# One hybrid decoder layer: GpSimd's instructions kept in the order of the program

## The chip, the cores and the metric

The kernel runs on one core of a Trainium2 chip. The metric is the device time of one execution in microseconds (us), lower is better. Its engines are TensorE (PE in the profile), VectorE (DVE), ScalarE (ACT), GpSimd (POOL) and SyncE (SP, which only issues transfers here). Each engine works through its own queue of instructions in order and waits where an instruction's semaphore is not there yet.

## The reference, cut to what matters

One layer on 256 tokens, model width 1024, in float32. A combined projection of the normed input gives group A's queries, keys and values (8 heads of 64) and group B's latents with a shared rotary key. Group A's queries and keys are normed by head, group B's after their up-projections, where 32 of 96 columns are rotated by the token's position.

```python
xn = rms_norm(h, norm_mix_g)
proj = jnp.einsum('bsd,de->bse', xn, w_in)
qa, ka, va, c_q, c_kv, k_rope = jnp.split(proj, cuts, axis=-1)
qa = rms_norm(qa.reshape(b, s, N_HEADS_A, HEAD_DIM_A), qnorm_a_g)
ka = rms_norm(ka.reshape(b, s, N_HEADS_A, HEAD_DIM_A), knorm_a_g)
out_a = dilated_attention(qa, ka, va, rel_bias).reshape(b, s, WIDTH_A)
...
kb = rms_norm(kb, knorm_b_g)
qb = jnp.concatenate([qb[..., :QK_NOPE_DIM], apply_rope(qb[..., QK_NOPE_DIM:], positions)], axis=-1)
kb = jnp.concatenate([kb[..., :QK_NOPE_DIM], apply_rope(kb[..., QK_NOPE_DIM:], positions)], axis=-1)
...
h = h + jnp.einsum('bse,ed->bsd', mixed, w_o)
hid = jnp.square(jax.nn.relu(jnp.einsum('bsd,df->bsf', hn, w_ff1)))
h = h + jnp.einsum('bsf,fd->bsd', hid, w_ff2)
```

## The kernel before

Every product is made of three: an operand is split into a high part, which TensorE takes exactly, and the rest (`his`, `los`), and high x high, low x high and high x low are summed in PSUM. For weights ScalarE writes the high part (L243) and DVE the low one (L244, called a split below), in pieces of up to 1024 columns, in rings of `PARTS` = 5 buffers; the weights come in by SyncE's queue into a ring of three `raw` buffers. Transposed activations are split in the same way with the norm's gain (L275, L276).

TensorE's order is written out by hand in `STEPS` and held by `keep_in_program_order`, which `Products._issue` calls for each product and transpose. A letter is a kind of step: `p` projects group A's queries and keys, `c0` and `c1` the query latent, `l` the key-value latent, `A` transposes and stacks group A's heads (`stack_heads`), `L` transposes the latents, `x` makes a unit of group A's scores and probabilities, `y` transposes one, `r` is the rotary tables. The other engines' instructions are put in order by a scheduler that simulates the timeline; only at the start, while `starting` is set, ScalarE's and DVE's are pinned too.

The work of GpSimd:

- fills of constants: `ident`, `mhalf` (L260), `causal` (L437, L438) and the zeros of `q_lo` (L447);
- the input's norm factor (`ssx`, `rstd`, `eps_x`, L358 to L363) and the products of gains `qk_a`, `qk_b`, which read `cols`;
- group A's four powers: `normed_heads` has ScalarE square a projection, DVE sum it by head (`head_sums`, L460, into `s_a`), GpSimd scale the sum (L484) and raise it to -1/2 (`rsqrt`, L266), and DVE multiply (L487). `s_a00` and `s_a01` belong to the queries, `s_a10` and `s_a11` to the keys, for the two halves of the tokens;
- the rotary tables (`rotary_tables`, L371 to L421): some 60 small operations on 32 or 64 columns, nearly all in one chain, with three on DVE in it (L398, L401, L403);
- later the latents' norm factors, the rotation of the shared key (L616 is its last step), and group B's powers.

`stack_heads` for the keys ends on DVE with L506, which frees the PSUM bank (`mm`, two of them) that the transposes of the next step need. L501 is the same for the queries, L540 the division of group A's probabilities.

Of the kernel before, what the change touches and what calls it, by code (L numbers as in the profile page):

```python
# [16 lines left out]
F32 = mybir.dt.float32  # L17
F32R = mybir.dt.float32r
I32 = mybir.dt.int32
AF = mybir.ActivationFunctionType  # L20
ALU = mybir.AluOpType
AX = mybir.AxisListType

P = 128
S = 256
# [3 lines left out]
H = 8  # L29
DA = 64  # L30
# [13 lines left out]
MASK = 1e29  # L44
# [104 lines left out]
class Products:  # L149


    def __init__(self, tc):
        self.tc = tc
        self.in_order = True
# [8 lines left out]
        return self._issue(self.tc.nc.tensor.transpose(**kw))  # L163


@with_exitstack
def tile_layer(ctx, tc, x, xt, cols_in, rows_in, w_all, out):
    nc = tc.nc
    V, A, G, T = nc.vector, nc.scalar, nc.gpsimd, Products(tc)

    const = ctx.enter_context(tc.tile_pool(name="const", bufs=1))
    keep = ctx.enter_context(tc.tile_pool(name="keep", bufs=1))
    big = ctx.enter_context(tc.tile_pool(name="big", bufs=2))
    two = ctx.enter_context(tc.tile_pool(name="two", bufs=3))
# [173 lines left out]
    load(out=rows, in_=rows_in)  # L348
    starting.clear()

    def sumsq(src, dst):
        junk = sqs.tile([P, DM], mybir.dt.bfloat16, name="sqs")
        return A.activation(out=junk[:, :src.shape[1]], in_=src, func=AF.Square, accum_out=dst)  # L353

    ssx = tiny(NT, "ssx")
    for t in range(NT):
        sumsq(xs[t], ssx[:, t:t + 1])
# [75 lines left out]
        A.dma_start(out=vec_d, in_=vec)  # L433
        A.dma_start(out=bias_r, in_=bass.AP(tensor=vec_d.tensor, offset=vec_d.offset, ap=[[1, P], [NDIST, H], [1, S]]))

    causal = const.tile([P, S], F32, name="causal")
    G.memset(causal, 0.0)  # L437
    G.affine_select(out=causal[:, P:], in_=causal[:, P:], pattern=[[-1, P]], compare_op=ALU.is_ge, fill=MASK, base=0, channel_multiplier=1)  # L438

    k_st = big.tile([P, H // 2, 2, S], F32R, name="big")
    q_st = two.tile([P, 2, H // 2, 2, S], F32R, name="two")
    q_hi, q_lo = q_st[:, 0], q_st[:, 1]
    own = (slice(0, DA), slice(DA, P))
    for i in range(2):
        G.memset(q_lo[own[1 - i], :, i, :].bitcast(F32), 0.0)  # L447
    va, vb = ([keep.tile([P, H, DV], F32, name=f"{n}{t}") for t in range(NT)] for n in ("va", "vb"))


# [133 lines left out]
    def have_cq(b, ps):  # L584
        for t in range(NT):
            V.tensor_copy(out=cn[t][:, b * 384:(b + 1) * 384], in_=ps[t][:, :384])
            sumsq(cn[t][:, b * 384:(b + 1) * 384], ssc[:, b * NT + t:b * NT + t + 1])
# [6 lines left out]
    def have_ckv(ps):  # L594
        for t in range(NT):
            V.tensor_copy(out=cn[t][:, QR:], in_=ps[t][:, :KVR])
            V.tensor_copy(out=kr[t], in_=ps[t][:, KVR:KVR + ROPE])
            sumsq(cn[t][:, QR:], ssc[:, 2 * NT + t:2 * NT + t + 1])
            sumsq(kr[t], ssc[:, 3 * NT + t:3 * NT + t + 1])

        G.tensor_tensor(out=ssc[:, NT:2 * NT], in0=ssc[:, 0:NT], in1=ssc[:, NT:2 * NT], op=ALU.add)
        for i, n in enumerate((QR, KVR)):
            sl = slice(i * NT, (i + 1) * NT)
            G.tensor_scalar(out=mc[:, sl], in0=ssc[:, (i + 1) * NT:(i + 2) * NT], scalar1=1.0 / n, scalar2=None, op0=ALU.mult)
            G.tensor_tensor(out=mc[:, sl], in0=mc[:, sl], in1=eps_x, op=ALU.add)
        rsqrt(fc, mc, 2 * NT)
        G.tensor_scalar(out=eps_q, in0=mc[:, 0:NT], scalar1=EPS, scalar2=None, op0=ALU.mult)
        G.tensor_tensor(out=by_kr, in0=rstd, in1=rstd, op=ALU.mult)
        G.tensor_tensor(out=add_k, in0=ssc[:, 3 * NT:], in1=by_kr, op=ALU.mult)
        G.tensor_scalar(out=add_k, in0=add_k, scalar1=1.0 / DB, scalar2=EPS, op0=ALU.mult, op1=ALU.add)  # L610
        G.tensor_tensor(out=add_k, in0=add_k, in1=m_kv, op=ALU.mult)
        G.tensor_tensor(out=by_kr, in0=m_kv, in1=f_kv, op=ALU.mult)
        G.tensor_tensor(out=by_kr, in0=by_kr, in1=rstd, op=ALU.mult)
        for t in range(NT):
            rotate(G, kr[t].unsqueeze(1), tabs[1], t)
            G.tensor_scalar(out=kr[t], in0=kr[t], scalar1=by_kr[:, t:t + 1], scalar2=None, op0=ALU.mult)  # L616
# [108 lines left out]
    for step in STEPS.split():  # L725
        name, _, times = step.partition("*")
# [137 lines left out]
```

## Time and profile before

| what | us |
|---|---|
| three runs | 324.32, 325.64, 325.48 |
| their median | 325.48 |
| the profiled execution | 324.74 |
| its span, first to last instruction | 322.9 |
| TensorE busy | 311.2 |
| DVE busy | 216.0 |
| ScalarE busy | 177.7 |
| GpSimd busy | 62.5 |

Times in the views are counted from the span's start. A busy share is a mean over the whole span; which wait ends last in a stretch is read from the waits and from the order of time in that stretch.

### The profile page before, as it was taken

What the parts mean: (1) busy time and instruction counts of PE and PEld (TensorE: products, weight loads), DVE (VectorE), ACT (ScalarE), POOL (GpSimd) and SP (SyncE); (2) the same over time, 40 slices, a digit from 0 to 9 for tenths busy, and PEclk for the clock granted to TensorE, in tenths of its full rate; (3) what the DMA queues carried; (4) which work ended last, traced back from release to release, by engine and by line L of the source; (5) the groups of instructions that cost most, each with busy time, mean ns of one, the idle gap of its engine ahead of it and who ended that gap; (6) DMA issues with size and microseconds to landing.
All of it is one profiled execution on the core that took longest, in us unless ns stands there. A gap on an engine that the chain in (4) does not pass through costs nothing.

```text
span 322.9 us, 4547 instructions
## 1 busy us (share of the span) xinstructions
PE 311.2 (96%) x1646; PEld 266.1 (82%) x1646; DVE 216.0 (67%) x387; ACT 177.7 (55%) x317; POOL 62.5 (19%) x118
## 2 busy tenths in 40 slices
PE   8989779989999999999999999999999999999995
PEld 7867679968998887788888888888888888888883
DVE  4673869986887997357887484574764845845722
ACT  5866246977885677328674463453544544535500
POOL 6889960170336200000200000000000000000000
PEclk9999997999999999999999999999999999999999
DMA  7994748434461473212848556465637364563002
GB/s 241 405 346 149 253 112 300 154 116 132 144 202 62 137 255 130 80 52 74 319 144 296 212 151 239 164 219 156 239 134 256 137 211 179 169 222 130 0 35 97
DMA packets 12326, 56.95 MB, mean 176 GB/s; under 512 B 1384, under 2 KB 3440, under 8 KB 7696
## 3 DMA queue, kind: packets, MB, share of 16 engines
q1 hardware_dynamic: 10560, 54.94, 49.4%
q10 hardware_dynamic: 1744, 1.73, 1.8%
q8 instruction: 13, 0.21, 0.2%
q14 instruction: 9, 0.07, 0.1%
HBM read 55.07 MB, written 1.06 MB: 174 GB/s over the span
## 4 chain that ended last, share of the span: by engine, by line
PE 76%; POOL 11%; DVE 4%; ACT 3%; issue 2%; DMA 1%; DVEq 0%; ACTq 0%; POOLq 0%
PE acc L160 40%; PE sc L160 17%; PE mm L160 14%; PE mm L163 4%; POOL rot L380 3%; POOL s_a L266 2%; ACT his L243 2%; DVE los L244 2%; DMA first<-in_xt_dram 1%; POOL ang L381 1%; ACT sqs L353 1%; POOL trig L381 1%; DVE two L276 1%; ACT two L275 1%; POOL rstd L266 1%
## 5 line engine op out<-in xcount | busy, mean ns | idle before, releaser
L244 DVE TENSOR_TENSOR los<-raw,his 128x1024 fp32r<-128x1024 f32 (+3 forms) x106 | 121.4, 1153 | 60.4 <-ACT his L243 60.3
L243 ACT CAST his<-raw 128x1024 fp32r<-128x1024 f32 (+3 forms) x106 | 104.2, 991 | 88.1 <-PE acc L160 43.6
L160 PE MATMUL acc<-his,two 128*128 128x512 f32 (+2 forms) x288 | 73.7, 378 | 0.0
L160 PE MATMUL acc<-two,his 128*128 128x512 f32 x240 | 63.1, 393 | 0.2 <-DVE half L773 0.2
L160 PEld LDWEIGHTS acc<-his,two 128*128 128x128 f32 x288 | 51.5, 192 | 6.6 <-issue 0.8
L160 PE MATMUL mm<-his,big 128*128 128x512 f32 x128 | 49.1, 390 | 0.0
L160 PE MATMUL sc<-his,big 128*128 128x512 f32 x128 | 49.1, 390 | 0.0
L160 PEld LDWEIGHTS acc<-two,his 128*128 128x128 f32 x240 | 42.7, 189 | 7.6 <-DVE half L773 0.4
L160 PE MATMUL acc<-los,two 128*128 128x512 f32 (+2 forms) x144 | 41.3, 368 | 1.0 <-DVE los L244 1.0
L160 PEld LDWEIGHTS acc<-two,los 128*128 128x128 f32 x240 | 34.6, 190 | 3.4
L160 PE MATMUL acc<-two,los 128*128 128x256 f32 x240 | 35.9, 282 | 0.0
L160 PEld LDWEIGHTS acc<-los,two 128*128 128x128 f32 x144 | 26.5, 190 | 5.0 <-DVE los L244 1.4
L160 PEld LDWEIGHTS mm<-his,big 128*128 128x128 f32 x128 | 24.1, 188 | 4.8
L160 PEld LDWEIGHTS sc<-his,big 128*128 128x128 f32 x128 | 24.1, 188 | 4.7
L160 PE MATMUL sc<-los,big 128*128 128x512 f32 x64 | 24.9, 390 | 0.0
L160 PE MATMUL mm<-los,big 128*128 128x512 f32 x64 | 24.9, 390 | 0.0
L537 ACT ACTIVATE half<-half,mx 128x128 f32<-128x128 f32 (+1 forms) x32 | 14.2, 449 | 2.7 <-DVE mx L534 2.7
L163 PE MATMUL mm<-ident,half 128*128 128x128 f32 x64 | 10.5, 286 | 4.7 <-DVE two L501 2.2
L163 PEld LDWEIGHTS mm<-ident,half 128*128 128x128 f32 x64 | 7.9, 142 | 7.6 <-issue 4.4
L160 PEld LDWEIGHTS mm<-los,big 128*128 128x128 f32 x64 | 12.0, 188 | 2.5
L160 PEld LDWEIGHTS sc<-los,big 128*128 128x128 f32 x64 | 12.0, 188 | 2.5
L772 ACT COPY half<-acc 128x256 f32<-128x256 f32 x30 | 9.7, 373 | 7.9 <-PE acc L160 7.9
(148 smaller groups left out, 325.6 us busy)
## 6 DMA issues: line engine op xcount, KB each, us to landing
raw<-in_weights_dram SPq DMA_DIRECT2D x36, 1024.0 KB, 4.8
raw<-in_weights_dram SPq DMA_DIRECT2D x13, 512.0 KB, 5.9
raw<-in_weights_dram SPq DMA_DIRECT2D x6, 768.0 KB, 4.5
raw<-in_weights_dram SPq DMA_DIRECT2D x2, 576.0 KB, 3.9
x<-in_x_dram SPq DMA_DIRECT2D x2, 512.0 KB, 8.7
big<-vec_d ACTq DMA_DIRECT2D x1, 1024.0 KB, 5.1
big<-in_xt_dram SPq DMA_DIRECT2D x3, 256.0 KB, 6.7
raw<-in_weights_dram SPq DMA_DIRECT2D x2, 384.0 KB, 2.8
```

The source lines that it names most:

```text
L160: return self._issue(self.tc.nc.tensor.matmul(**kw))
L163: return self._issue(self.tc.nc.tensor.transpose(**kw))
L243: pinned(A.copy(out=hi, in_=raw))
L244: pinned(V.tensor_tensor(out=lo, in0=raw, in1=hi.bitcast(F32), op=ALU.subtract))
L266: G.tensor_tensor(out=out, in0=in_, in1=mhalf[:, :n], op=ALU.pow)
L275: a = pinned(A.activation(out=hi, in_=src, func=AF.Copy, scale=g))
L276: v = pinned(V.scalar_tensor_tensor(out=lo, in0=src, scalar=g, in1=hi.bitcast(F32), op0=ALU.mult, op1=ALU.subtract))
L353: return A.activation(out=junk[:, :src.shape[1]], in_=src, func=AF.Square, accum_out=dst)
L380: G.tensor_scalar(out=tmp, in0=in0, scalar1=scalar, scalar2=None, op0=op0)
L381: G.tensor_tensor(out=out, in0=tmp, in1=in1, op=op1)
L537: A.activation(out=sb[:, i, :], in_=sb[:, i, :], func=AF.Exp, scale=-1.0, bias=mx[:, i:i + 1], accum_out=mx[:, 4 + i:5 + i])
L772: A.copy(out=zs, in_=ps[2 * b + i][:, S:])
```

## The change

A wrapper, `InOrder`, takes the place of `nc.gpsimd`: each GpSimd instruction that the kernel issues through it is kept in program order, as TensorE's are. The fills of `causal` and `q_lo` move up in the program, ahead of the input's norm factor. The program's text decides the rest: the tables (step `r0`) are written behind both calls of `normed_heads`. In the changed file all these GpSimd instructions carry line 174, and lines behind the wrapper are higher by 11 to 23 (L398 is L421, L401 L424, L403 L426, L487 L499, L506 L518).

```diff
+class InOrder:
+
+
+    def __init__(self, tc, engine):
+        self.tc, self.engine = tc, engine
+
+    def __getattr__(self, name):
+        op = getattr(self.engine, name)
+        return lambda *a, **kw: self.tc.keep_in_program_order(op(*a, **kw))
+
+
 @with_exitstack
 def tile_layer(ctx, tc, x, xt, cols_in, rows_in, w_all, out):
     nc = tc.nc
-    V, A, G, T = nc.vector, nc.scalar, nc.gpsimd, Products(tc)
+    V, A, G, T = nc.vector, nc.scalar, InOrder(tc, nc.gpsimd), Products(tc)
...
     load(out=cols, in_=cols_in)
     load(out=rows, in_=rows_in)
     starting.clear()
+
+    causal = const.tile([P, S], F32, name="causal")
+    G.memset(causal, 0.0)
+    G.affine_select(out=causal[:, P:], in_=causal[:, P:], pattern=[[-1, P]], compare_op=ALU.is_ge, fill=MASK, base=0, channel_multiplier=1)
+
+
+
+    q_st = two.tile([P, 2, H // 2, 2, S], F32R, name="two")
+    q_hi, q_lo = q_st[:, 0], q_st[:, 1]
+    own = (slice(0, DA), slice(DA, P))
+    for i in range(2):
+        G.memset(q_lo[own[1 - i], :, i, :].bitcast(F32), 0.0)
...
-    causal = const.tile([P, S], F32, name="causal")
-    G.memset(causal, 0.0)
-    G.affine_select(out=causal[:, P:], in_=causal[:, P:], pattern=[[-1, P]], compare_op=ALU.is_ge, fill=MASK, base=0, channel_multiplier=1)
-
-
-
     k_st = big.tile([P, H // 2, 2, S], F32R, name="big")
-    q_st = two.tile([P, 2, H // 2, 2, S], F32R, name="two")
-    q_hi, q_lo = q_st[:, 0], q_st[:, 1]
-    own = (slice(0, DA), slice(DA, P))
-    for i in range(2):
-        G.memset(q_lo[own[1 - i], :, i, :].bitcast(F32), 0.0)
```

GpSimd's queue before, where the powers of group A's queries stand (`trig` and `rot2` are the tables' polynomial, `s_a` the sums by head):

```order
L381 TENSOR_TENSOR trig_611<-rot2_620,sq_610 128x64
L484 TENSOR_SCALAR s_a00_323<-s_a00_323,eps_x_206 128x8
L380 TENSOR_SCALAR rot2_623<-trig_611 128x64
L266 TENSOR_TENSOR s_a00_323<-s_a00_323,mhalf_119 128x8
L381 TENSOR_TENSOR trig_611<-rot2_623,sq_610 128x64
L484 TENSOR_SCALAR s_a01_331<-s_a01_331,eps_x_206 128x8
L380 TENSOR_SCALAR rot2_626<-trig_611 128x64
L266 TENSOR_TENSOR s_a01_331<-s_a01_331,mhalf_119 128x8
L381 TENSOR_TENSOR trig_611<-rot2_626,sq_610 128x64
```

The same place now, from the products of gains to the first operations of the tables (`ang0` to `ang3` are the angles):

```order
L174 TENSOR_SCALAR qk_b_249<-qk_b_249 128x1
L174 TENSOR_SCALAR s_a00_323<-s_a00_323,eps_x_214 128x8
L174 TENSOR_TENSOR s_a00_323<-s_a00_323,mhalf_119 128x8
L174 TENSOR_SCALAR s_a01_331<-s_a01_331,eps_x_214 128x8
L174 TENSOR_TENSOR s_a01_331<-s_a01_331,mhalf_119 128x8
L174 TENSOR_SCALAR s_a10_384<-s_a10_384,eps_x_214 128x8
L174 TENSOR_TENSOR s_a10_384<-s_a10_384,mhalf_119 128x8
L174 TENSOR_SCALAR s_a11_392<-s_a11_392,eps_x_214 128x8
L174 TENSOR_TENSOR s_a11_392<-s_a11_392,mhalf_119 128x8
L174 TENSOR_TENSOR ang0_562<-pos_566,first_107 128x32
L174 TENSOR_SCALAR ang1_563<-ang0_562 128x32
```

The four powers stood among the second half of the tables; now they follow each other with nothing between them, and the whole of the tables stands behind the fourth.

DVE's queue before, at the end of the start (`los` are splits, `ang` and `arg` belong to the tables, `two` is the transposed input):

```order
L244 TENSOR_TENSOR los<-raw,his 128x1024
L276 SCALAR_TENSOR_TENSOR two<-big,first,two 128x256 x2
L398 SCALAR_TENSOR_TENSOR ang_565<-ang_562 128x32
L244 TENSOR_TENSOR los<-raw,his 128x1024
L276 SCALAR_TENSOR_TENSOR two<-big,first,two 128x256
L401 TENSOR_TENSOR ang_562<-ang_562,ang_565 128x32
L244 TENSOR_TENSOR los<-raw,his 128x1024
L403 TENSOR_TENSOR arg<-ang_562,ang_565 128x2x16
```

DVE's queue now, where these three operations stand (`two<-mm` is group A's queries, `big<-mm` its keys, `nats` the latent):

```order
L513 SCALAR_TENSOR_TENSOR two<-mm,qk_a,two 64x4x128 x2
L598 COPY nats<-sc 128x384 x2
L255 TENSOR_TENSOR los<-raw,his 128x576 x3
L421 SCALAR_TENSOR_TENSOR ang_565<-ang_562 128x32
L424 TENSOR_TENSOR ang_562<-ang_562,ang_565 128x32
L518 TENSOR_TENSOR big<-mm,big 64x4x128
L426 TENSOR_TENSOR arg<-ang_562,ang_565 128x2x16
L518 TENSOR_TENSOR big<-mm,big 64x4x128
```

The tables' three operations on DVE moved from the splits of the first projection to the stacking of group A's keys.

## Rows read from the trace of the kernel before

**Rows 1.** The page: busy us of each engine, share of the span, instructions.

```profile
PE 311.2 (96%) x1646; PEld 266.1 (82%) x1646; DVE 216.0 (67%) x387; ACT 177.7 (55%) x317; POOL 62.5 (19%) x118
```

**Rows 2.** TensorE's waits, 16 to 60 us: who for whom, total us, times, longest.

```profile
PE mm L163 <- DVE two L501: 2.2, 1, 2.2
PE mm L163 <- DVE half L487: 1.1, 1, 1.1
PE acc L160 <- DVE los L244: 1.0, 1, 1.0
PE sc L160 <- DVE los L244: 0.9, 1, 0.9
```

**Rows 3.** Windows: stretch, length, busy us of PE, PEld, DVE, ACT, POOL, PE clock.

```profile
50.00:52.00 2.00, 2.00 (x9) 2.00 (x8) 1.97 (x5) 1.92 (x6) 0.00 (x0) 0.50 0.91 385
52.00:54.00 2.00, 2.00 (x10) 2.00 (x9) 1.94 (x4) 1.98 (x5) 0.00 (x0) 0.71 0.59 164
```

**Rows 4.** DVE's waits, 10 to 60 us.

```profile
DVE half L487 <- POOL s_a L266: 9.5, 3, 5.0
DVE ang L398 <- POOL ang L381: 2.6, 1, 2.6
```

**Rows 5.** GpSimd in order of time: start, length, line, operation [idle before].

```profile
5.19 0.40 POOL L375 TENSOR_TENSOR ang<-pos,first 128x32 f32<-128x32 f32 x1 [1.37 <-DVE pos L371]
...
16.51 0.59 POOL L381 TENSOR_TENSOR ang<-rot,ang 128x32 f32<-128x32 f32 x2
...
29.44 0.28 POOL L484 TENSOR_SCALAR s_a<-s_a,eps_x 128x8 f32<-128x8 f32 x1
...
30.15 1.68 POOL L266 TENSOR_TENSOR s_a<-s_a,mhalf 128x8 f32<-128x8 f32 x1
...
33.63 2.22 POOL L266 TENSOR_TENSOR s_a<-s_a,mhalf 128x8 f32<-128x8 f32 x1
```

**Rows 6.** DVE in order of time, 12 to 50 us.

```profile
17.13 0.19 DVE L398 SCALAR_TENSOR_TENSOR ang<-ang 128x32 f32<-128x32 f32 x1 [2.62 <-POOL ang L381]
...
22.48 0.69 DVE L460 TENSOR_REDUCE s_a<-sqs 128x8 f32<-128x512 f32 x1 [0.74 <-ACT sqs L459]
...
31.87 0.69 DVE L487 TENSOR_TENSOR half<-acc,s_a 128x512 f32<-128x512 f32 x1 [4.98 <-POOL s_a L266]
32.48 1.86 DVE L244 TENSOR_TENSOR los<-raw,his 128x768 fp32r<-128x768 f32 x2
```

**Rows 7.** The transfer of the gains: its issue, and KB and us to landing.

```profile
11.32 0.33 SPq L220 DMA_DIRECT2D cols<-in_cols_dram  x1
...
cols<-in_cols_dram SPq DMA_DIRECT2D x1, 42.0 KB, 8.7
```

**Rows 8.** DVE in order of time, 49 to 60 us.

```profile
50.52 2.10 DVE L244 TENSOR_TENSOR los<-raw,his 128x576 fp32r<-128x576 f32 x3
52.65 1.28 DVE L506 TENSOR_TENSOR big<-mm,big 64x512 fp32r<-64x512 f32 x2
...
54.75 1.30 DVE L506 TENSOR_TENSOR big<-mm,big 64x512 fp32r<-64x512 f32 x2
...
59.48 0.87 DVE L276 SCALAR_TENSOR_TENSOR two<-mm,cols,two 128x256 fp32r<-128x256 f32 x2
```

**Rows 9.** TensorE in order of time, 54 to 70 us.

```profile
56.33 0.82 PE L163 MATMUL mm<-ident,nats 128*128 128x128 f32 x6
...
68.11 0.82 PE L163 MATMUL mm<-ident,half 128*128 128x128 f32 x4 [1.35 <-DVE half L540]
```

**Rows 10.** GpSimd in order of time, end of the shared key and the next step.

```profile
72.35 0.71 POOL L616 TENSOR_SCALAR kr<-kr,by_kr 128x32 f32<-128x32 f32 x2
86.22 0.27 POOL L670 TENSOR_SCALAR s_k<-s_k,add_k 128x4 f32<-128x4 f32 x1 [13.16 <-DVE s_k L460]
```

**Rows 11.** A GpSimd power and a DVE split that meet, 86 to 112 us.

```profile
87.97 1.08 POOL L266 TENSOR_TENSOR s_k<-s_k,mhalf 128x4 f32<-128x4 f32 x1
...
88.31 0.95 DVE L244 TENSOR_TENSOR los<-raw,his 128x768 fp32r<-128x768 f32 x1
```

## Prediction

> **What bounds the kernel.** I read the page's busy shares first, then TensorE's (PE's) waits, then the waits of VectorE (DVE), and last the two engines' order of time. The reader is to see that TensorE is busy 96% of the span [rows 1] and that its idle time from 16 to 60 us is four waits, all put down to DVE: 1.0, 0.9, 1.1 and 2.2 us, 5.2 together [rows 2]. Behind the longest of them TensorE's granted clock is at 0.50, its 1.2 GHz level, from 50 to 52 us and at 0.71 on average from 52 to 54 [rows 3]. That costs 2 x 0.50 + 2 x 0.29 = 1.6 us. Its work is in a fixed order, so 5.2 + 1.6 = 6.8 us is the most that can be won here.
>
> DVE is late because it waits itself: 9.5 us for the powers of group A's norm (L487) and 2.6 us for the rotary angles (L398), 12.1 in all [rows 4]. The sum for the first power, s_a00, begins at 22.48 and takes 0.69 [rows 6]. GpSimd (POOL) starts on it only at 29.44 [rows 5], since it is busy with the tables, and the product that needs it runs at 31.87 [rows 6].
>
> **The change, step by step.** I keep the line numbers of before; in the changed file the DVE lines 398, 401, 403, 487 and 506 are 421, 424, 426, 499 and 518, and GpSimd's operations all show line 174.
>
> *The fills* stay at the start in both orders. They cost nothing.
>
> *DVE's waits at the angles leave the beginning.* L398 stood there ahead of a split and held it for 2.6 us, and TensorE waited 1.0 us for that split [rows 2, 4]. With the wait gone the projection ends about 1.0 us earlier.
>
> *A wait is added in front of the powers:* qk_a reads the gains, and the four powers now stand behind it. That transfer was issued at 11.32 and took 8.7 us to land, so at 20.0 [rows 7]. The first sum comes at 22.48 + 0.69 - 1.0 = 22.17 [rows 6], so the wait ends 2.2 us sooner than it could hurt. I cost it at nothing.
>
> *The powers come at once.* A scale takes 0.28 and a power 1.68 where nothing disturbs it, and 2.22 where a DVE split (L244) was running beside its start [rows 5, 6]. I let one split of 0.93 (two took 1.86 [rows 6]) stand in the way: s_a00 is done at 22.17 + 0.28 + 1.68 + 0.93 = 25.1, against its product at 31.87 in the old order. DVE then does the product (0.69) and two splits (1.86) and is at 27.6. The second power was done at 25.06 + 1.96 = 27.0, so DVE doesn't wait. After the second product (28.3) it has two splits, a sum, a split, a sum, at 0.93 and 0.69 each, which brings it to 32.5. The third sum is ready at 28.3 + 1.86 + 0.69 = 30.85, its power behind another split at 30.85 + 1.96 + 0.93 = 33.7. The fourth follows it at 33.74 + 1.96 = 35.7. None of the first three waits of TensorE is left, and the fourth has no cause of its own any more.
>
> *The tables begin only now,* at 35.7, and DVE has three small operations in them, 0.19 us each [rows 6]. L398 needs the first 25 operations of the tables, which ran from 5.19 to 17.10 before: 11.9 us, or 0.48 each [rows 5]. Two undisturbed ones take 0.59 together [rows 5], so 25 x 0.30 = 7.5 is the lower end, and the rest was lost beside splits. I take 11.9, because DVE has four splits in this stretch too. L398 can then start at 35.7 + 11.9 = 47.6. L401 comes two GpSimd operations later: 0.19 for L398, 2 x 0.48 for the two and 0.19 for L401 itself, so it ends near 48.95.
>
> *What waits behind L398.* In the new order L398 stands behind the three 576-column splits and directly ahead of L506, which writes group A's low keys and frees the PSUM banks that TensorE's next transposes fill. L506 began at 52.65 before [rows 8]. It now begins at 48.95 instead, and L403, one more operation of 0.19, is put in behind the first of them, so what follows comes 52.65 - 48.95 - 0.19 = 3.5 us sooner. DVE itself could be there at 52.62 - 12.1 = 40.5 if nothing else held it, or at 52.62 - 6.8 = 45.8 if it keeps step with TensorE [rows 8]; so a wait of 2 to 7 us has moved here from the powers. It is what takes back half of the 6.8.
>
> *From there to the end.* Up to the pair of L276 at 59.48 DVE has no gap before either [rows 8]. TensorE's transposes at 56.33 followed the last L506 (54.75 + 1.30 = 56.05) by 0.3 us, and at 68.11 TensorE waited 1.35 us for DVE's L540 [rows 8, 9]. DVE thus leads through this stretch, and TensorE moves with it by 3.5 us. If its clock falls once more in the new wait, the 1.6 us fall in the time that it would wait at 68.11 anyway.
>
> *The end of GpSimd's queue.* The tables have to be done for the keys' shared rotary part, which ended at 72.35 + 0.71 = 73.1 before; the next GpSimd step came at 86.22, after 13.16 us of idle time [rows 10]. A delay of up to 13 us is covered there.
>
> **Sum.** The profiled execution took 324.74 us, 1.84 over its span. 324.74 - 3.5 = 321.2 us. The median of the three runs is 325.48, 0.74 higher, so the same gain read from the median would be 322.0. I stay with 321.2.
>
> **A rule weighed against the rows.** A split that began at 88.31, inside a GpSimd power that ran from 87.97 for 1.08 us, took 0.95 us [rows 11], as a split does elsewhere (1.86 for two [rows 6]). So GpSimd loses where they meet and DVE does not. The Trainium skill (SBUF — State Buffer, "Who interferes with whom") says that a DVE instruction with two SBUF inputs and a GpSimd instruction that reads SBUF share a port, and that the one that started first blocks the other fully. By that rule the split at 88.31 should have waited, and the trace does not show it; the stretched power, 2.22, agrees with it. By the rows the sum is 321.2, by the rule it is the fourth rival below.
>
> **The rivals.**
> *The tables are quick enough.* If nothing disturbs the 25 operations, L398 is ready at 35.7 + 7.5 = 43.2 and DVE, in step with TensorE at 45.8, doesn't wait. Then the full 6.8 us are won: 317.9 us. For it: GpSimd runs undisturbed while DVE waits. Against it: the four splits.
> *The tables eat the gain.* If the first L506 starts between 50.9 and 54.1, the change is under 1.6 us either way. It takes 2 us more on the way to L398: a scale that comes late, or splits that meet more of the operations. About 324 us.
> *Slower: one operation behind the other.* In the old order the table's operations went in pairs that don't need each other; in program order each waits for the result before it. The gain is gone when L398 is ready at 47.6 + 3.5 = 51.1, that is at 15.4 us for the 25 operations or 0.62 us each. At 0.70 each it would be 17.5 us and the kernel 2.1 us slower: 326.8. Against it: undisturbed operations that follow each other take 0.30 each [rows 5].
> *A power holds up a split.* If a split that begins during a power had to wait for its end, the split behind the first product, which begins at 25.06 + 0.69 = 25.75, would wait until 27.02, 1.3 us, and push the fourth power, and with it the tables, back by as much: 322.5 us. Against it: the split in [rows 11]. By the rule of the Trainium skill above it would be so.
> *The keys come late.* Only if the tables end 13 us later than planned [rows 10].
>
> **How the numbers follow.** A measurement of this kernel tells apart about 0.5%, 1.6 us. My forecast, 319 to 323 us, has 0.57; quick tables 0.15; the power that holds up a split 0.05; the gain eaten 0.13; slower by serial operations 0.08; late keys 0.02. Faster by over 0.5% is 0.57 + 0.15 + 0.05 = 0.77, the same 0.14, slower 0.09, with late keys shared between the last two. The range reaches from the quick tables, 317.9, to the middle of the eaten gain with the median's distance, 324.9. It leaves out about 0.1 at the top and 0.08 below.
>
> **What would show it.** Right: s_a00's product near 25 instead of 31.87; no wait of DVE for a power over 1 us; one wait of DVE of 2 to 7 us for GpSimd at the line of L398, ending near 48, and a second of about 1 us behind it; TensorE's three early waits gone and a new one at the transposes ahead of the latent's normalised columns, with a low clock after it perhaps. The first of the L506 operations should start near 49. Wrong: DVE doesn't wait at L398 at all, or L398 starts after 51; a split stretched beyond 1.3 us beside a power; or TensorE waiting for something after 75 us that it didn't wait for before.

## The result, and the profile after the change

The changed kernel takes 320.16 us in the median of four runs (319.68 to 320.45), the kernel before 325.50 beside it. The ratio is 0.9842, with a 95% interval from 0.9817 to 0.9868: 5.3 us or 1.6% faster. The forecast was 321.2 with a range from 317.9 to 324.9. The profiled execution took 320.45 us with a span of 318.6; before it was 324.74 and 322.9, so this pair is 4.3 us apart. The missing microsecond between 4.3 and 5.3 is cleared up below.

TensorE's work is the same, its share of the shorter span is higher (the page of the changed kernel; compare [rows 1]):

```profile
PE 311.2 (98%) x1646; PEld 266.8 (84%) x1646; DVE 215.7 (68%) x387; ACT 177.9 (56%) x317; POOL 57.8 (18%) x118
```

The four waits of [rows 2] are gone, and the one at 68.11 of [rows 9] has shrunk from 1.35 to 0.5. One new wait stands for L518 (L506 before). TensorE's waits, 10 to 80 us (who for whom, total us, times, longest):

```profile
PE mm L163 <- DVE big L518: 1.8, 1, 1.8
PE mm L163 <- DVE half L552: 0.5, 1, 0.5
```

DVE's 9.5 us for the powers have become 0.6; its wait for the angles is still there, at another place (DVE's waits, same stretch; compare [rows 4]):

```profile
DVE ang L421 <- POOL ang L174: 2.9, 1, 2.9
...
DVE ang L424 <- POOL ang L174: 0.6, 1, 0.6
DVE half L499 <- POOL s_a L174: 0.6, 2, 0.4
```

GpSimd in order of time shows why: the powers come as soon as their sums do, and the tables start behind the fourth (start, length, line, operation, idle before; compare [rows 5]):

```profile
22.89 0.28 POOL L174 TENSOR_SCALAR s_a<-s_a,eps_x 128x8 f32<-128x8 f32 x1 [0.53 <-DVE s_a L472]
23.25 2.54 POOL L174 TENSOR_TENSOR s_a<-s_a,mhalf 128x8 f32<-128x8 f32 x1
...
26.26 1.64 POOL L174 TENSOR_TENSOR s_a<-s_a,mhalf 128x8 f32<-128x8 f32 x1
31.29 0.91 POOL L174 TENSOR_SCALAR s_a<-s_a,eps_x 128x8 f32<-128x8 f32 x1 [3.39 <-DVE s_a L472]
32.28 1.64 POOL L174 TENSOR_TENSOR s_a<-s_a,mhalf 128x8 f32<-128x8 f32 x1
...
34.37 1.64 POOL L174 TENSOR_TENSOR s_a<-s_a,mhalf 128x8 f32<-128x8 f32 x1
35.97 0.24 POOL L174 TENSOR_TENSOR ang<-pos,first 128x32 f32<-128x32 f32 x1
...
37.42 0.98 POOL L174 TENSOR_TENSOR ang<-rot,ang 128x32 f32<-128x32 f32 x1
...
38.85 0.25 POOL L174 TENSOR_TENSOR ang<-rot,ang 128x32 f32<-128x32 f32 x1
...
43.20 0.81 POOL L174 TENSOR_TENSOR ang<-rot,ang 128x32 f32<-128x32 f32 x1
...
46.52 0.25 POOL L174 TENSOR_TENSOR ang<-rot,ang 128x32 f32<-128x32 f32 x1
```

The first product by a power (L499) runs at 25.83 where it ran at 31.87 [rows 6]. Then DVE gets as far as the angles, waits 2.92 us and 0.64 us, and everything behind is 4.3 to 4.8 us earlier than in [rows 8] (DVE in order of time):

```profile
25.83 0.69 DVE L499 TENSOR_TENSOR half<-acc,s_a 128x512 f32<-128x512 f32 x1 [0.20 <-POOL s_a L174]
26.43 1.82 DVE L255 TENSOR_TENSOR los<-raw,his 128x768 fp32r<-128x768 f32 x2
...
43.13 0.76 DVE L255 TENSOR_TENSOR los<-raw,his 128x576 fp32r<-128x576 f32 x1 [0.87 <-ACT his L254]
46.81 0.19 DVE L421 SCALAR_TENSOR_TENSOR ang<-ang 128x32 f32<-128x32 f32 x1 [2.92 <-POOL ang L174]
47.65 0.19 DVE L424 TENSOR_TENSOR ang<-ang,ang 128x32 f32<-128x32 f32 x1 [0.64 <-POOL ang L174]
47.87 0.69 DVE L518 TENSOR_TENSOR big<-mm,big 64x512 fp32r<-64x512 f32 x1
...
50.31 1.30 DVE L518 TENSOR_TENSOR big<-mm,big 64x512 fp32r<-64x512 f32 x2
...
55.03 0.87 DVE L287 SCALAR_TENSOR_TENSOR two<-mm,cols,two 128x256 fp32r<-128x256 f32 x2
```

The first L518 began 52.65 - 47.87 = 4.8 us earlier, the pair L287 59.48 - 55.03 = 4.45, the span ended 4.3 earlier. TensorE had been idle for 1.8 us at 51.15, and behind that its granted clock is at 0.50, the 1.2 GHz level, in one window and lower on average in the next (stretch, length, busy us of PE, PEld, DVE, ACT, POOL, clock):

```profile
52.00:54.00 2.00, 2.00 (x10) 2.00 (x10) 1.97 (x4) 1.70 (x4) 1.83 (x3) 0.50 0.47 190
54.00:58.00 4.00, 4.00 (x29) 4.00 (x28) 3.69 (x9) 2.90 (x7) 3.58 (x6) 0.85 0.42 127
```

### The profile page after: what moved, and what is told of

Read it like the earlier page. It is cut to its first block, busy times and chain, and to the rows that moved or that the text cites. A ratio compares the mean times of both kernels' runs of the same rounds, so it can differ in the third digit from the quotient of the medians.

```text
span 318.6 us, 4545 instructions
## 1 busy us (share of the span) xinstructions
PE 311.2 (98%) x1646; PEld 266.8 (84%) x1646; DVE 215.7 (68%) x387; ACT 177.9 (56%) x317; POOL 57.8 (18%) x118
## 4 chain that ended last, share of the span: by engine, by line
PE 83%; DVE 5%; POOL 5%; ACT 3%; issue 2%; DVEq 0%; ACTq 0%
PE acc L160 45%; PE sc L160 19%; PE mm L160 15%; PE mm L163 4%; DVE los L255 2%; POOL s_a L174 2%; POOL ang L174 2%; ACT his L254 2%; POOL rot L174 1%; ACT sqs L376 1%; DVE big L518 1%; DVE s_a L472 0%; DVE two L287 0%; DVE half L785 0%; ACT two L286 0%
## 5 line engine op out<-in xcount | busy, mean ns | idle before, releaser
L788 ACT CAST big<-half 128x512 fp32r<-128x512 f32 x16 | 10.0, 625 | 4.1 <-DVE half L786 4.1
L785 DVE TENSOR_TENSOR half<-acc,half 128x256 f32<-128x256 f32 x30 | 11.4, 418 | 1.3 <-ACT half L784 1.3
## 6 DMA issues: line engine op xcount, KB each, us to landing
big<-vec_d ACTq DMA_DIRECT2D x1, 1024.0 KB, 11.9
```

The lines of the kernel that those rows point to most:

```text
L785: V.tensor_tensor(out=zs, in0=ps[2 * b + i][:, 0:S], in1=zs, op=ALU.add)
L788: A.copy(out=ht[:, sl, :], in_=s3)
```

## The experiments

The theory behind the prediction is called A in what follows: what counts is where DVE, which takes its queue in order, waits for GpSimd, and what stands behind the waiting operation. The rivals bear other letters, and each expectation says what its rival is. In the lines shown below the line numbers of DVE's operations shift by up to four between these kernels; their names (`big`, `ang`, `two`, `half`) stay.

**The fills alone.** `causal` and `q_lo` move up in the program as in the change, but GpSimd isn't wrapped and stays with the scheduler.

```diff
-    V, A, G, T = nc.vector, nc.scalar, InOrder(tc, nc.gpsimd), Products(tc)
+    V, A, G, T = nc.vector, nc.scalar, nc.gpsimd, Products(tc)
```

> Only the fills' place in the program is changed; the order of GpSimd is the scheduler's again. Theory A: nothing that DVE waits for has moved, so the time is that of the kernel before, 325 us, within 0.5 us, with s_a00's power at about 30 us. Rival C (the earlier fills, or something at the start, give part of the gain): between 320 and 325.

Measured: 325.12 us, a ratio to the kernel before of 1.0003 (95% interval 0.9992 to 1.0015; the ratios below are meant in the same way). DVE's waits for the powers (9.5) and at the angles (2.6) are those of before. The fills are no part of the gain.

**The tables ahead of the powers.** Program order is kept, but the step of the tables goes to the front of the program.

```diff
-STEPS = """p*13 b0 p*3 c0*4 A0 c0*4 c1*5 A1 r0 c1*3 l*2 L0 ...
+STEPS = """r0 p*13 b0 p*3 c0*4 A0 c0*4 c1*5 A1 c1*3 l*2 L0 ...
```

> GpSimd in program order as in the change, but the tables are written ahead of the projection, so they stand in front of the four powers instead of behind them. Theory A: tables from 22.3 to 47.8 us, s_a00's power done near 49.8 and s_a01's near 51.8, so TensorE's first transposes come near 52 instead of 33.4, 19 us late, of which later waits give back some 3.5; a low clock behind so long an idle stretch adds 1 to 2. About 337 us. Rival B (program order by itself is the gain): about 320 us.

Measured: 336.58 us, ratio 1.0355 (1.0320 to 1.0390). The first power now waits for the whole of the tables (GpSimd in order of time, then TensorE's waits):

```profile
47.88 1.68 POOL L174 TENSOR_TENSOR s_a<-s_a,mhalf 128x8 f32<-128x8 f32 x1
```

```profile
PE mm L163 <- DVE half L499: 18.0, 2, 17.0
```

So program order as such wins nothing. With the tables in front, 11.4 us are lost, over twice what the change gains.

**Half of the tables in GpSimd's idle time.** In the change GpSimd stands idle before the input's norm. The first 25 operations go there, the rest stays behind the powers.

```diff
+        yield
         arg = const.tile([P, NT, 2, HR], F32, name="arg")
...
+    rotary = rotary_steps()
+    next(rotary)
...
-        "r": lambda i: rotary_tables(),
+        "r": lambda i: next(rotary),
```

> GpSimd in program order, with the tables' first 25 operations in its idle stretch between the fills and the input's norm factor (4 to 19 us), the rest behind the powers. The scheduler then places L398 back among the first splits, and L401 and L403 behind group A's queries. Theory A: DVE waits about 2.6 us for L398 near 17 us again, which costs TensorE 1.0 us as it did before, but none of the three operations stands ahead of L506 with its result still missing, so the 1.8 us wait and its low clock go: about 318 us. Rival B: as the changed kernel, 320.

Measured: 317.91 us, ratio 0.9774 (0.9750 to 0.9797). DVE waits at the angles again where it did before, 2.9 us at 17.57, and TensorE 1.2 us behind it, but nothing waits at the stacking of the keys: the first eviction is at 45.70.

**The tables' work taken off DVE.** The three operations are done by GpSimd in other forms (|a| as 2 max(a, 0) - a, and so on).

```diff
-        V.scalar_tensor_tensor(out=r, in0=a0, scalar=-1.0, in1=a0, op0=ALU.mult, op1=ALU.max)
+        G.tensor_scalar(out=r, in0=a0, scalar1=0.0, scalar2=2.0, op0=ALU.max, op1=ALU.mult)
+        G.tensor_tensor(out=r, in0=r, in1=a0, op=ALU.subtract)
...
```

> The changed kernel, but the tables' three DVE operations are computed on GpSimd (absolute value, minimum and maximum by a scalar maximum and an add or subtract), so DVE waits for the tables nowhere. Theory A (DVE's queue leads: the wait of 2.9 us at L421 and 0.6 at L424 stands ahead of the L518 that frees TensorE's banks): L518 starts near 44.7 instead of 47.87, TensorE's wait of 1.8 us at the latent's transposes and the low clock behind it go, and the time falls by about 3 us, to 317. Rival B (what counts is that GpSimd's chain runs without being taken apart, not who waits for it): same as the changed kernel, 320, or a little more for five GpSimd operations more.

Measured: 316.94 us, ratio 0.9740 (0.9721 to 0.9759). GpSimd's tables end later than in the change and DVE does not notice. The evictions run as soon as ScalarE's copy is there (DVE in order of time), and TensorE's clock stays at 1.00 from 44 to 64 us:

```profile
44.70 1.28 DVE L521 TENSOR_TENSOR big<-mm,big 64x512 fp32r<-64x512 f32 x2 [0.97 <-ACT big L520]
```

**Both together.** The half in the idle time and the tables' work off DVE.

```diff
+    rotary = rotary_steps()
+    next(rotary)
...
-        V.scalar_tensor_tensor(out=r, in0=a0, scalar=-1.0, in1=a0, op0=ALU.mult, op1=ALU.max)
+        G.tensor_scalar(out=r, in0=a0, scalar1=0.0, scalar2=2.0, op0=ALU.max, op1=ALU.mult)
+        G.tensor_tensor(out=r, in0=r, in1=a0, op=ALU.subtract)
...
```

> Both of the gains together: the first 25 operations of the tables in GpSimd's idle time ahead of the powers (5.5 to 17.5 us), the rest behind the powers, and the tables' operations of DVE done by GpSimd. Theory A: DVE never waits for the tables in either, so an earlier end of them is worth nothing more: as with the tables taken off DVE alone, 316.9 us within 0.5. Rival B (each microsecond that the tables end earlier counts): at least 1 us below 316.9, as the cosines end several microseconds earlier.

Measured: 316.64 us, ratio 0.9743 (0.9728 to 0.9757). No more than with the tables taken off DVE alone, although the tables are done some ten microseconds earlier (the last product of the sines and cosines begins at 47.94 in place of 58.91). Where DVE doesn't wait for them, their end is worth nothing by itself.

**The place alone.** GpSimd's queue is the change's, to the last operation. DVE's first operation of the tables is only put behind the last eviction of the keys.

```diff
+    evictions = []
...
+        with tc.issue_after(evictions[-1].ins):
-        V.scalar_tensor_tensor(out=r, in0=a0, scalar=-1.0, in1=a0, op0=ALU.mult, op1=ALU.max)
+            V.scalar_tensor_tensor(out=r, in0=a0, scalar=-1.0, in1=a0, op0=ALU.mult, op1=ALU.max)
...
-                    V.tensor_tensor(out=k_st[other, :, i, ts], in0=t3[rs], in1=k_st[rs, :, i, ts].bitcast(F32), op=ALU.subtract)
+                    evictions.append(V.tensor_tensor(out=k_st[other, :, i, ts], in0=t3[rs], in1=k_st[rs, :, i, ts].bitcast(F32), op=ALU.subtract))
```

> GpSimd's queue exactly as in the change; DVE's three operations of the tables alone are moved, from ahead of the four evictions of the keys (L518) to behind the last of them. Theory A (DVE's place): the evictions begin near 44.6 us in place of 47.9, as with the tables taken off DVE, the angles are there before DVE comes to them or within 1 us, and the time is 317.5 us, between 316.9 (no table work on DVE) and 318. Rival B (what GpSimd's chain ends at sets the time): no change against the changed kernel, 320.2.

Measured: 316.64 us, ratio 0.9749 (0.9735 to 0.9763), against 0.9847 (0.9834 to 0.9861) for the changed kernel measured beside it. Here the order is turned round: the evictions first, the angles behind them, and no wait for the angles at all (DVE in order of time).

```profile
44.82 1.28 DVE L520 TENSOR_TENSOR big<-mm,big 64x512 fp32r<-64x512 f32 x2 [0.97 <-ACT big L519]
...
46.95 1.30 DVE L520 TENSOR_TENSOR big<-mm,big 64x512 fp32r<-64x512 f32 x2
48.28 0.19 DVE L423 SCALAR_TENSOR_TENSOR ang<-ang 128x32 f32<-128x32 f32 x1
```

GpSimd waits for DVE instead (1.53 us for L423 and 1.77 for the next), and can afford to. It is the best version, level with the two before it, by an ordering alone and with no work changed.

**A longer chain, behind and ahead.** Two kernels have a fill and ten small operations more on GpSimd ahead of the tables. In the first the scheduler itself puts DVE's three operations behind the evictions; in the second they are held ahead of them.

```diff
+        spare = const.tile([P, NT * HR], F32, name="spare")
+        G.memset(spare, 1.0)
+        for _ in range(10):
+            G.tensor_scalar(out=spare, in0=spare, scalar1=1.0, scalar2=None, op0=ALU.mult)
```

The second has this as well:

```diff
-... c0*4 A0 c0*4 c1*5 A1 r0 c1*3 l*2 L0 ...
+... c0*4 A0 c0*4 c1*5 r0 A1 c1*3 l*2 L0 ...
...
+        tc.keep_in_program_order(V.scalar_tensor_tensor(out=r, in0=a0, scalar=-1.0, in1=a0, op0=ALU.mult, op1=ALU.max))
...
```

> The changed kernel with a fill and ten small chained operations more on GpSimd ahead of the tables (by 0.38 us each, estimated from the rows of 32 columns, some 3.8 us), and DVE's three operations of the tables behind the four evictions of the 64x512 sums in place of ahead of them. GpSimd's 25 operations then end near 35.97 + 3.8 + 10.8 = 50.5 us in place of 46.8. Theory A (what counts is who stands behind DVE's wait on its in-order engine): the first eviction begins near 44.7 us as soon as its sum is there, DVE still waits about 2 us for the angles at its new place, the pair of products of 0.87 us begins near 53.6 us in place of 55.0, and the time is about 318.8 us, below the changed kernel's 320.2 although the chain is longer. Rival B (the length of GpSimd's chain sets the time wherever DVE stands): about 3.5 us above the changed kernel, 323.7.

> The same ten operations more on GpSimd as in the run with them behind the evictions, so the same chain to about 50.5 us, but DVE's three operations of the tables held ahead of all four evictions (and two splits and two copies moved ahead by the scheduler). Theory A: the first eviction begins near 53.3 us in place of 44.5, TensorE's transposes wait until about 56 in place of 51.2 in the changed kernel, the time is 322 to 326 us. Rival (the place does not count, the length of the chain alone): the same 318.7 as with the ten operations behind the evictions.

Measured: 318.69 us behind the evictions, ratio 0.9806 (0.9790 to 0.9821), and 326.54 us ahead of them, ratio 1.0052 (1.0039 to 1.0065). The first is DVE in order of time with the three behind:

```profile
44.45 1.28 DVE L522 TENSOR_TENSOR big<-mm,big 64x512 fp32r<-64x512 f32 x2 [0.97 <-ACT big L521]
...
50.57 0.19 DVE L425 SCALAR_TENSOR_TENSOR ang<-ang 128x32 f32<-128x32 f32 x1 [1.61 <-POOL ang L174]
```

The second with the three ahead:

```profile
50.44 0.19 DVE L425 SCALAR_TENSOR_TENSOR ang<-ang 128x32 f32<-128x32 f32 x1 [2.54 <-POOL ang L174]
...
52.71 0.19 DVE L430 TENSOR_TENSOR arg<-ang,ang 128x32 f32<-128x32 f32 x1 [0.33 <-POOL ang L174]
52.93 0.68 DVE L522 TENSOR_TENSOR big<-mm,big 64x512 fp32r<-64x512 f32 x1
```

TensorE's waits in the second:

```profile
PE mm L163 <- DVE big L522: 8.1, 2, 7.1
```

The angles come at nearly the same time in both (50.57 and 50.44), DVE's first wait for them is longer by only 0.9 us in the second, and 7.85 us lie between the two times. At the same length of the chain, what stands behind the wait decides. The length is not nothing: with the three behind the evictions, ten operations more cost 2.05 us against the place alone (318.69 and 316.64), since DVE then waits 1.61 and 0.41 us there, ahead of two splits and the pair L287.

Beside the place one thing differs between the two: the scheduler also moved two splits and two copies. One of these splits, 1.23 us at 53.65, now stands between the first eviction and the second, so a microsecond or so of the 7.85 may be its. The second run came out half a microsecond above its expected range. TensorE's clock, which I had not put in, is at 0.50 from 54 to 62 us there; that this is the reason was not tested.

**The change once more,** beside the last two, with no edit.

> The changed kernel once more, on the same chip as the two runs beside it: 320.2 within 0.5 us. In the profiled execution TensorE's first group of products (his, at 5.4 us) tells whether the 0.9 us by which it began later than before belongs to the order of GpSimd (then 7.3 us for the first low product again) or to how the first transfers land (then anything from 6.4 to 7.3).

Measured: 319.87 us, ratio 0.9847 (0.9834 to 0.9861), a second time 5.0 us. Its trace settles the microsecond left over above. TensorE in order of time, first in the trace of the change:

```profile
2.61 3.19 PE L160 MATMUL sc<-half 128*128 128x256 f32 x9
5.46 2.05 PE L160 MATMUL acc<-his,two 128*128 128x512 f32 x4
7.31 0.67 PE L160 MATMUL acc<-los,two 128*128 128x512 f32 x2
```

Then the same kernel in this run:

```profile
2.61 2.65 PE L160 MATMUL sc<-half 128*128 128x256 f32 x9
5.24 1.18 PE L160 MATMUL acc<-his,two 128*128 128x512 f32 x4
6.27 0.73 PE L160 MATMUL acc<-los,two 128*128 128x512 f32 x2
```

And the kernel before:

```profile
6.44 0.62 PE L160 MATMUL acc<-los,two 128*128 128x512 f32 x2
```

In the first the low product came 1.04 us later, without a wait in front of it: TensorE itself was slower there. It runs one product behind the other in both traces, and the four products ahead of the low one, of the same shape, take 2.05 us in place of 1.18. From the second of the four on they begin every 0.43 us in the first trace and every 0.23 in the second, as at 1.2 and 2.4 GHz. The traces' records of the granted clock begin, at 1.00, at 7.39 us in the first and at 4.54 in the second; the view of windows counts the time ahead of a record as 1.00 and doesn't show this. So TensorE's clock rose later in the first, which is neither of the two that the expectation names. GpSimd's order does not decide it: with the fills alone, in the scheduler's order, the low product came at 7.25, with the order otherwise as before. Nor does the landing of the first transfer, as the place alone shows: DVE's first operation on the input ran at 4.73 there and at 4.74 here, but its low product came at 7.30:

```profile
5.46 2.01 PE L160 MATMUL acc<-his,two 128*128 128x512 f32 x4
7.30 0.62 PE L160 MATMUL acc<-los,two 128*128 128x512 f32 x2
```

The span of the repeated run is 317.6, 1.0 less than in the first trace of the change. Against a nearly equal start (6.44 and 6.27) the gain is therefore 322.9 - 317.6 = 5.3 us, as the medians have it.

## Why the prediction was right, and where its sizes were off

*The fills cost nothing:* shown by the run with them alone.

*DVE's waits at the angles leave the beginning, TensorE 1.0 us earlier:* right, with a start like that of before: in the second trace of the change the first sum began at 21.20 in place of 22.48 [rows 6], 1.1 us sooner when the 0.17 between the starts is taken off. The worth depends on the start. Where the start was late, TensorE waited there for 0.4 us only (the run with the fills alone) against 1.0 [rows 2]. In the profiled execution the first sum's scale came at 22.89; in the second trace of the change it came at 22.00, close to the 22.17 forecast.

*The wait in front of the powers costs nothing:* right. The products of gains ran at 21.40 to 22.36, ahead of the first sum.

*The powers come at once:* right in kind, slightly pessimistic. With an equal start (the second trace) the first product ran at 24.93 against 25.1 forecast for its power. The fourth power was done at 33.47 + 1.64 = 35.1 against 35.7.

*The 25 operations take 11.9 us:* this is the term that was mis-sized. They took from 35.97 to 46.77, 10.8 us or 0.43 each, and 10.8 again in the second trace. Undisturbed ones come every 0.35 us, counting the gap to the next: the 0.59 of [rows 5] holds two operations but only one gap, so the lower end was 8.6 us and not 7.5. Four splits began in the stretch (37.34, two from 40.83, 43.13), and at each of them one operation is long: 0.98 and 0.81 in place of 0.25 above, and two more between them; together they lost 2.2 us. I had carried over the loss of the old place because I counted four splits in both; the old one had six (at 5.40, 6.31, two from 7.67, 10.47 and 12.49 in the trace of before). The two operations between L398 and L401 and the two DVE ones themselves took 46.81 to 47.84, 1.03 us, where I had 1.35 for them.

*What waits behind L398:* right, and the core of it. DVE's wait of 2 to 7 us came out as 2.92 and a second of 0.64 where I expected about 1. DVE was ready for L398 at 43.9 (43.0 in the second trace), between the 40.5 and the 45.8 of the forecast. The first L506 came at 47.87 in the profiled execution against 48.95, and with an equal start at 46.96, so the forecast was 2.0 us late there: 0.6 from the powers, 1.1 from the 25 operations, 0.3 from the rest. That makes 3.5 + 2.0 = 5.5 against the 5.3 measured.

*From there to the end:* right. All the marks moved together, and the low clock was hidden, as the two traces of the change show. With the same wait (1.78 and 1.76 us) the clock fell to 0.50 in one and stayed at 1.00 in the other. The one with the full clock (its window 52 to 54 us, then its waits) has in its place longer waits for DVE later:

```profile
52.00:54.00 2.00, 2.00 (x19) 2.00 (x17) 2.00 (x2) 1.97 (x6) 1.92 (x2) 1.00 0.01 4
```

```profile
PE mm L163 <- DVE big L518: 1.8, 1, 1.8
PE mm L163 <- DVE half L552: 1.0, 1, 1.0
PE mm L163 <- DVE two L287: 0.8, 1, 0.8
```

Those two are 1.3 us longer together, and past the difference in the start the spans agree. The same pair exists for the kernel before: the run with the fills alone waited 2.3 us for the queries, kept its clock at 1.00 from 50 to 54 us, and took 325 us like the kernel with the fall [rows 3]. DVE led this stretch, so the clock cost nothing.

*The end of GpSimd's queue is covered:* right. Its next step after the shared key came after 10.17 us of idle time, and TensorE's only wait after 75 us is one of 0.2 us, in the trace of before as in that of the change.

*6.8 us is the most that can be won:* wrong. Three versions win 8.2 to 8.4 us in the medians. What was left out shows when the profiled executions of before and of the place alone are set side by side (the latter's page, then its wait at the place of [rows 9]):

```profile
PE 309.2 (98%) x1646; PEld 265.5 (84%) x1646; DVE 215.6 (68%) x387; ACT 177.9 (56%) x317; POOL 58.6 (19%) x118
```

```profile
PE mm L163 <- DVE half L554: 1.0, 1, 1.0
```

The span went from 322.9 to 315.4, 7.5 us. TensorE's waits make up 5.6 of it: the 5.2 of [rows 2], and 0.35 of the 1.35 us at 68.11 [rows 9], which I had taken as DVE's lead, to be there in any case; 1.0 of it did stay. TensorE's busy time, 311.2 [rows 1] and 309.2, makes up the other 2.0, against the 1.6 that I had put down to the clock; the 0.4 between them was not taken apart. The rest up to 8.2 is the choice of executions: the profiled one of the place alone is the slowest of its four, 317.21 against a median of 316.64. Nor are the waits and the clock two separate gains, since by the pair above the waits are longer where the clock doesn't fall. DVE's own lateness is one number for both: its first eviction went from 52.65 to 44.82 with the place alone, 7.8 us.

**The rivals.** That the tables are quick enough fell: DVE did wait, 2.9 us, of which the 2.2 lost beside the four splits are the larger part. That the tables eat the gain fell too: the first L506 came at 47.87, and not between 50.9 and 54.1. That a power holds up a split fell: the split of 1.82 us for two at 26.43 above began inside the power of 26.26 to 27.90 and took no longer than elsewhere, and neither did one inside the third power (DVE in order of time):

```profile
32.56 0.95 DVE L255 TENSOR_TENSOR los<-raw,his 128x768 fp32r<-128x768 f32 x1
```

The other direction holds: a split ran from 23.03 to 24.25, and the power that began at 23.25 took 2.54, 0.90 more than 1.64. The Trainium skill (SBUF — State Buffer, "Who interferes with whom") has whichever of the two started first block the other fully. The trace agrees where DVE was first, and differs where GpSimd's power was.

The slower rival fell as it was put: the operations took 0.43 us each where it needed 0.62. Its turning point, L506 no earlier than before, is real all the same, and the run with ten operations more ahead of the evictions passes it: its first eviction is at 52.93, against 52.65 before, and its time 1.7 us above that of before. By the start of its first eviction the change is some five microseconds away from that.

## What to carry to other kernels

When a chain on one engine is moved, look for its few operations on another, in-order engine: they decide, by what is queued behind them; the chain's length counts only as far as they wait for it. Count the cost of such a wait from the first operation behind it that frees a buffer of the bound engine, and put the waiting operations behind that one; here that was worth another 3.2 us beyond the change (316.64 against 319.87) with nothing else touched. Size a moved chain by what runs beside it at its new place.

## What the runs showed of the hardware beyond this

Two executions of one program with the same wait of TensorE, 1.76 and 1.78 us, were granted different clocks behind it, 1.00 and 0.50, and past the difference in their start their spans agree; so a fall of the clock in one trace need not be a cost.

TensorE's clock also rises at another time in each execution: at 4.54 and 7.39 us in two traces of the same program, with products one behind the other from 1.2 us on in both. The first low product moved with it, from 6.27 to 7.31 us, and the whole program with that. Two spans should be compared from a common mark when a microsecond matters.

An operation of GpSimd can stretch over more than one split. With the tables ahead of the powers, one of 0.25 us elsewhere took 4.01, and ended only behind four splits that followed each other (GpSimd, then DVE in order of time); what let it through in the end no run takes apart.

```profile
25.01 4.01 POOL L174 TENSOR_TENSOR ang<-rot,ang 128x32 f32<-128x32 f32 x1
```

```profile
25.37 3.54 DVE L255 TENSOR_TENSOR los<-raw,his 128x768 fp32r<-128x768 f32 x4
```
